# A macaron encoder block in exact split arithmetic: where the operands of down pieces stand among the weight sums, and which three pieces of one group make their sums in place

## The chip, the cores and the metric

The kernel runs on one core of one Trainium2 chip. The metric is the device time of one launch in microseconds. Three runs of the kernel before took 2424.29, 2424.43 and 2427.40 us; the median is 2424.43.

## The reference

One layer on a residual stream of 256 tokens by 2048 channels, all in float32:

```python
x = x + 0.5 * swiglu(rms_norm(x, ffn1_norm), ffn1_w_up, ffn1_w_down)
# HGRN2 and RG-LRU branches of one input projection, merged by gates
x = x + merged @ w_out
x = x + cross_attention(rms_norm(x, xattn_norm), rms_norm(mem, mem_norm), wq, wkv, wo)
x = x + 0.5 * swiglu(rms_norm(x, ffn2_norm), ffn2_w_up, ffn2_w_down)
return rms_norm(x, final_norm)
```

with `swiglu(h, w_up, w_down)`: `gate, up = split(h @ w_up)`, then `(silu(gate) * up) @ w_down`. The hidden width is 5632. The change is only in the two feed-forward blocks, called ffn1 and ffn2 below.

## The kernel before, in words

**Arithmetic.** A float32 product is computed from fp32r halves. Each weight piece of 128 x 2048 numbers (1 MB) is loaded into a `raw` tile and split: ACT copies it into the high part `h` (L138), and DVE subtracts that from `raw` into the low part `l` (L139). TensorE (PE) multiplies high by high (L547), high by the low part of the activations (L548) and low by high (L550).

**Pieces.** The hidden width is worked in 11 groups of 512. A group has eight up pieces, called pairs 0 to 7 by their place in the contraction (256 channels each: two blocks of 128, with four blocks of 512 weights in the piece: gate and up for each of the two). Most pairs use a Strassen-like scheme ("fast") with seven block products in place of eight. For it four *sums* of the weight blocks are needed as well: one operation on DVE for two of them (L285) and one for each of the others (L287, L288; each takes the result in front). They make a second tile `td`, which is split too, in two halves of 1024 columns: ACT writes `h`, DVE `tl`. A fast pair is thus 21 matmuls of 512 columns. When the products of a group are done, they are added up (L634 to L646), pass through silu (L580, L581) and are turned by PE into the operands `hidop` (L592 on ACT, L593 on DVE).

**Down pieces** multiply `hidop` by a 128 x 2048 piece of `w_down`, 24 matmuls each. From group 1 on, two or four of them stand behind each group's eight pairs. They are of kind "plain" (load at L270, split on ACT, split on DVE), but where four stand together the third is "added": it is loaded one piece earlier (L253), ACT writes its negative into `l` (L254), GpSimd's queue adds the weights to that by a DMA (L255), and ACT writes `h` (L263).

**Sums made ahead.** In ffn2, 58 of the pairs are "ready": their sums are made while the middle of the kernel runs (`make_ahead`: a load into `prep`, four subtractions on DVE, L200, and a store to DRAM), and ffn2 loads them as a second 1 MB transfer (L277) beside 768 KB of the piece itself (L275). Which pairs of a group still make their sums *in place* stands in `sums_ready`: in ffn2 group 3, the first behind the attention's last products with its own table entry, pairs 0, 5 and 7. The order of the pairs in each such group is 1, 3, 4, 0, 2, 5, 6, 7, so these are the 4th, 6th and 8th.

**What sets the order.** `weights` keeps two pieces prepared ahead of the one that PE multiplies, and calls `prepare` (from L258) for each. The statements are written in that order, and the recording layer then puts each engine's instructions into a list order of its own by the dependences. `tc.issue_after(x)` holds what is recorded inside it behind `x` in that order; on one engine that is only an order, not a wait. Buffers are few: 3 `raw` (and 2 `raw2` in ffn2, which take two loads of every five), 3 `h`, 3 `l`, and `wide` tiles (`td`, `tl` and the group's `ev` in ffn1). All loads go through SP's queue, each when its buffer is free.

In time, ffn1 runs from 0 to 700 us, the middle to 1723 us and ffn2 to 2416 us.

Of the kernel before, what the change touches and what calls it, by code (L numbers as in the profile page):

```python
# [69 lines left out]

def sums_ready(name, e):

    made = () if e[1] < 3 else (0, 5, 7) if e[1] % 2 else (0, 3, 5, 7)
    return name == "ffn2" and e[0] == "fast" and e[2] not in made


# [1 line left out]
def block_kernel(ctx: ExitStack, tc: tile.TileContext, xT, xin, memT, vec, gfin, bgate, lruw, wu1, wd1, win, wv,  # L78
# [55 lines left out]
    done = {}  # L134


    def split(h, l, raw):
        done["high"] = act.activation(h, raw, ACT.Copy).ins  # L138
        done["low"] = dve.tensor_tensor(out=l, in0=raw, in1=h.bitcast(F32), op=ALU.subtract).ins  # L139
# [5 lines left out]
    plan, ahead, made_ahead = [], [], []  # L145
# [74 lines left out]
    def weights(*key):  # L220
        while plan and len(ahead) < 2:
            i = next(planned)
            k, src, kind = plan.pop(0)
            if i == 0:
                in_turn.enter_context(tc.manual_schedule(engines={sp.engine, act.engine, dve.engine}))
            if i < len(head):
                head[i]()
            if plan and plan[0][2] == "added":
                begun.append(begin_added(plan[0][1]))
            ahead.append((k, prepare(src, kind, 4 if i < 4 else 1)))  # L230
            if i in rest:
                rest[i]()
            beside(i)
            if i == 7:
                in_turn.close()
        k, w = ahead.pop(0)
        assert k == key, (k, key)
        return w
# [16 lines left out]
        nc.gpsimd.dma_start(l, src, accum_op=ALU.add)  # L255
        return raw, l

    def prepare(src, kind, cuts=1):  # L258

        if kind == "added":  # L260
            raw, l = begun.pop(0)
            h = hp.tile([P, 2048], F32R, name="h", tag="h")
            done["high"] = act.activation(h, raw, ACT.Copy).ins  # L263
            return h, l
        raw = raw_tile()
        n = 2048 // cuts
        if kind == "plain":
            h, l = split_tiles()
            for a in range(0, 2048, n):
                sp.dma_start(raw[:, a:a + n], src[:, a:a + n])  # L270
                split(h[:, a:a + n], l[:, a:a + n], raw[:, a:a + n])
            return h, l
        if kind == "ready":
            src, t = src
# [14 lines left out]
        h, l = split_tiles()  # L289
# [10 lines left out]
            tl = lp.tile([P, 2048], F32R, name="tl", tag="l")  # L300
        for a in (0, 1024):
            split(th[:, a:a + 1024], tl[:, a:a + 1024], td[:, a:a + 1024])
        return (h, l), (th, tl)

    def product(xs, *ws, late=()):
# [1010 lines left out]
```

## Time and profile before

| what | value |
|---|---|
| three timed runs | 2424.29, 2424.43, 2427.40 us |
| profiled execution | 2427.28 us, of it the profile's span 2425.5 us |
| granted TensorE clock, mean | 0.998 |
| memory traffic | 684.31 MB, mean 282 GB/s |

The span is what the trace covers; the device time is 1.8 us longer. Rows of the order of time read: start in us, duration in us, engine, line, operation, output and inputs by the program's names, shapes, count, and in square brackets the idle time ahead of it with what ended it. Where several instructions follow each other alike, a row holds them together, and its duration is from the first start to the last end. A row that begins with a stretch (1873.00:1918.20) gives its length and the busy time with the count of instructions of PE, weight loads, DVE, ACT and GpSimd, then the mean granted clock, the busy share of the DMA engines and GB/s. Rows of transfers give the kilobytes of one and the median of the microseconds from issue to landing. Starts of PE instructions are pipelined: two matmuls overlap, so the pitch is the difference of starts.

### The profile page before, as it was taken

Reading aid. Unit: us, or ns where it says so; the run is one execution under the profiler, and the core shown is the slowest. Engines: PE = TensorE matmul, PEld = TensorE weight load, DVE = VectorE, ACT = ScalarE, POOL = GpSimd, SP = SyncE. Lnnn points to the kernel's source line nnn. Section 1 sums busy time; section 2 is a strip of 40 time slices with the busy share of each in tenths; the row PEclk is TensorE's granted clock in tenths of the full one; section 3 lists DMA queues with packets and bytes.
Section 4 is the critical chain, followed back from the end, with each engine's and each line's share of the span. In section 5 each row is a group of like instructions: output and inputs, shape, how many; then the busy total and the mean of one; then the engine's idle time right before and its main releaser. Section 6 shows DMA issues by size and latency. Waiting matters only on the chain.

```text
span 2425.5 us, 30763 instructions
## 1 busy us (share of the span) xinstructions
PE 2409.3 (99%) x12139; PEld 2013.6 (83%) x12139; DVE 2025.6 (84%) x2260; ACT 1455.0 (60%) x1485; POOL 102.2 (4%) x166
## 2 busy tenths in 40 slices
PE   9999999999999999999999999999999999999998
PEld 8888888888788888888888888888888788888887
DVE  7999999998876868779776788777789999999995
ACT  8567677777664454476434555445676666666664
POOL 0000000000000000000000000000000000000000
PEclk9999999999999999999999999999999999999999
DMA  7579999988858776778989889977798878787873
GB/s 294 195 229 287 272 272 270 275 269 268 266 183 323 268 289 241 294 289 323 346 313 349 310 332 354 335 272 263 264 343 308 285 266 293 273 286 276 294 273 144
DMA packets 102385, 684.31 MB, mean 282 GB/s; under 512 B 11361, under 2 KB 11617, under 8 KB 29281
## 3 DMA queue, kind: packets, MB, share of 16 engines
q1 hardware_dynamic: 78192, 518.68, 57.5%
q0 software_dynamic: 23328, 162.54, 22.4%
q8 instruction: 95, 1.56, 0.2%
q10 hardware_dynamic: 720, 1.13, 0.1%
q14 instruction: 50, 0.40, 0.0%
HBM read 619.39 MB, written 62.91 MB: 281 GB/s over the span
## 4 chain that ended last, share of the span: by engine, by line
PE 91%; DVE 3%; DMA 3%; ACT 1%; issue 1%; ACTq 0%; DVEq 0%; SPq 0%
PE acc L547 16%; PE acc L548 16%; PE acc L550 16%; PE acc L313 11%; PE acc L338 8%; PE acc L341 8%; PE acc L339 8%; PE acc L316 6%; DMA raw<-wd 2%; DVE tl L139 1%; ACT h L138 1%; DVE l L139 1%; PE acc L588 1%; PE acc L477 1%; DMA t<-prep 0%
## 5 line engine op out<-in xcount | busy, mean ns | idle before, releaser
L138 ACT ACTIVATE h<-raw 128x2048 fp32r<-128x2048 f32 (+3 forms) x578 | 870.5, 1531 | 620.2 <-PE acc L339 189.6
L139 DVE TENSOR_TENSOR l<-raw,h 128x2048 fp32r<-128x2048 f32 (+2 forms) x406 | 837.3, 2065 | 187.6 <-ACT h L138 186.1
L547 PE MATMUL acc<-h,xh 128*128 128x512 f32 x1241 | 485.2, 392 | 2.7 <-ACT h L138 2.4
L548 PE MATMUL acc<-h,xl 128*128 128x512 f32 x1241 | 483.0, 390 | 0.0
L338 PE MATMUL acc<-h,ops 128*128 128x512 f32 x832 | 326.8, 393 | 0.0
L339 PE MATMUL acc<-h,ops 128*128 128x512 f32 x832 | 324.5, 390 | 0.0
L547 PEld LDWEIGHTS acc<-h,xh 128*128 128x128 f32 x1241 | 233.3, 188 | 56.2 <-ACT h L138 8.0
L547 PE MATMUL acc<-h,hidop 128*128 128x512 f32 x704 | 276.5, 393 | 2.3 <-ACT h L138 2.2
L313 PE MATMUL acc<-ops,h 128*128 128x512 f32 x1152 | 278.2, 393 | 0.0
L548 PE MATMUL acc<-h,hidop 128*128 128x512 f32 x704 | 274.8, 390 | 0.0
L548 PEld LDWEIGHTS acc<-h,xl 128*128 128x128 f32 x1241 | 233.3, 188 | 47.5
L313 PEld LDWEIGHTS acc<-ops,h 128*128 128x128 f32 x1152 | 211.7, 188 | 41.6
L139 DVE TENSOR_TENSOR tl<-raw,h 128x1024 fp32r<-128x1024 f32 x172 | 203.7, 1220 | 14.9 <-ACT h L138 14.5
L341 PE MATMUL acc<-l,ops 128*128 128x512 f32 x832 | 205.8, 389 | 0.0
L550 PE MATMUL acc<-l,hidop 128*128 128x512 f32 x704 | 189.3, 389 | 0.0
L138 ACT ACTIVATE h<-td 128x1024 fp32r<-128x1024 f32 x126 | 131.3, 1057 | 92.9 <-PE acc L548 42.3
L341 PEld LDWEIGHTS acc<-l,ops 128*128 128x128 f32 x832 | 156.2, 188 | 32.4
L338 PEld LDWEIGHTS acc<-h,ops 128*128 128x128 f32 x832 | 156.2, 188 | 32.2
L339 PEld LDWEIGHTS acc<-h,ops 128*128 128x128 f32 x832 | 156.3, 188 | 31.5
L139 DVE TENSOR_TENSOR tl<-td,h 128x1024 fp32r<-128x1024 f32 x126 | 152.0, 1220 | 31.2 <-ACT h L138 31.0
L200 DVE TENSOR_TENSOR prep<-prep 128x512 f32<-128x512 f32 x232 | 159.7, 689 | 20.9 <-DMA prep<-wu 17.1
L550 PE MATMUL acc<-l,xh 128*128 128x512 f32 x645 | 176.4, 389 | 0.0
(242 smaller groups left out, 2739.4 us busy)
## 6 DMA issues: line engine op xcount, KB each, us to landing
raw<-wu SPq DMA_DIRECT2D x114, 1024.0 KB, 6.3
raw<-wd SPq DMA_DIRECT2D x88, 1024.0 KB, 6.3
prep<-wu POOLq DMA_DIRECT2D x58, 1024.0 KB, 7.8
t<-prep POOLq DMA_DIRECT2D x58, 1024.0 KB, 7.8
raw<-t SPq DMA_DIRECT2D x58, 1024.0 KB, 6.9
raw<-wu SPq DMA_DIRECT2D x58, 768.0 KB, 5.0
raw<-win SPq DMA_DIRECT2D x40, 1024.0 KB, 4.8
raw<-wg SPq DMA_DIRECT2D x32, 1024.0 KB, 6.1
```

Source lines behind the costliest of these rows:

```text
L138: done["high"] = act.activation(h, raw, ACT.Copy).ins
L139: done["low"] = dve.tensor_tensor(out=l, in0=raw, in1=h.bitcast(F32), op=ALU.subtract).ins
L200: dve.tensor_tensor(out=b[o], in0=b[x], in1=b[y], op=ALU.subtract)
L313: pe.matmul(acc, h[:, k * P:(k + 1) * P], xs[k], start=k == 0, stop=False)
L316: done["product"] = pe.matmul(acc[:, :T], l[:, k * P:(k + 1) * P], xs[k][:, :T], start=False, stop=k == KT - 1).ins
L338: pe.matmul(accs[t], x[:, t * P:][:, :P], h[j], start=first and j == 0, stop=False)
L339: pe.matmul(accs[t], x[:, T + t * P:][:, :P], h[j], start=False, stop=False)
L341: done["product"] = pe.matmul(accs[t], x[:, t * P:][:, :P], l[j], start=False, stop=last and j == 3).ins
L477: pe.transpose(acc[:, z * T + t * P:][:, :P], tile[:, t * 512 + (2 * y + z) * P:][:, :P], ident)
L547: pe.matmul(acc, ah, bh, start=start, stop=False)
L548: pe.matmul(acc, al, bh, start=False, stop=False)
L550: pe.matmul(acc, ah, bl, start=False, stop=stop)
```

## The change

The first part is a table entry. In group 3 of ffn2 the pairs 2, 4 and 6 make their sums in place (the 3rd, 5th and 7th), and 0, 5 and 7 have theirs made ahead. The number of sums made ahead stays at 58.

The second part is an order. `prepare` remembers, at the end of each piece with sums, the ACT instruction that splits the second half of these sums. The split of a plain down piece is then held behind the latest such instruction. "Added" down pieces are not touched, nor are loads.

```diff
 def sums_ready(name, e):
-    made = () if e[1] < 3 else (0, 5, 7) if e[1] % 2 else (0, 3, 5, 7)
+    made = () if e[1] < 3 else (2, 4, 6) if e[1] == 3 else (0, 5, 7) if e[1] % 2 else (0, 3, 5, 7)
     return name == "ffn2" and e[0] == "fast" and e[2] not in made
...
-            ahead.append((k, prepare(src, kind, 4 if i < 4 else 1)))
+            ahead.append((k, prepare(src, kind, 4 if i < 4 else 1, k[1] == "down")))
...
-    def prepare(src, kind, cuts=1):
+    def prepare(src, kind, cuts=1, down=False):
...
                 sp.dma_start(raw[:, a:a + n], src[:, a:a + n])
-                split(h[:, a:a + n], l[:, a:a + n], raw[:, a:a + n])
+                with tc.issue_after(done["sums"]) if down else ExitStack():
+                    split(h[:, a:a + n], l[:, a:a + n], raw[:, a:a + n])
             return h, l
...
         for a in (0, 1024):
             split(th[:, a:a + 1024], tl[:, a:a + 1024], td[:, a:a + 1024])
+        done["sums"] = done["high"]
         return (h, l), (th, tl)
```

Lines below the edit in `prepare` stand one or two lower in the changed kernel (L634 is L636 there); the split stays at L138 and L139.

**ACT at the end of an ffn1 group.** The rows are the ACT splits of the last two pairs of the first group that has an "added" down piece behind it (`td` is a tile of sums, a `raw` of 2048 a down piece), up to that added piece (L254). Before:

```order
L138 ACTIVATE h<-td 128x1024 x3
L138 ACTIVATE h<-raw 128x1536
L138 ACTIVATE h<-td 128x1024
L138 ACTIVATE h<-raw 128x2048
L138 ACTIVATE h<-td 128x1024
L138 ACTIVATE h<-raw 128x2048
L634 ACTIVATE ev<-acc 128x512
L254 ACTIVATE l<-raw 128x2048
```

and after:

```order
L138 ACTIVATE h<-td 128x1024 x3
L138 ACTIVATE h<-raw 128x1536
L138 ACTIVATE h<-td 128x1024 x2
L138 ACTIVATE h<-raw 128x2048 x2
L636 ACTIVATE ev<-acc 128x512
L254 ACTIVATE l<-raw 128x2048
```

The second half of the last sums has moved ahead of the first down piece; nothing else moved here. On DVE the low part of the down piece likewise stands behind both `tl` splits.

**PE at the end of ffn2 groups 4 to 10.** The rows are the last pair's products (`xh`, `xl` are halves of the activations; `l` and `tl` the low parts of its weights and of its sums) and the first of a down piece (`hidop`). Before:

```order
L550 MATMUL acc<-l,xh 128x512 x3
L550 MATMUL acc<-tl,xh 128x512 x2
L547 MATMUL acc<-h,hidop 128x512
L548 MATMUL acc<-h,hidop 128x512
L547 MATMUL acc<-h,hidop 128x512
L547 MATMUL acc<-h,xh 128x512
L548 MATMUL acc<-h,xl 128x512
L547 MATMUL acc<-h,xh 128x512
L548 MATMUL acc<-h,xl 128x512
L548 MATMUL acc<-h,hidop 128x512
```

and after:

```order
L552 MATMUL acc<-l,xh 128x512 x2
L549 MATMUL acc<-h,xh 128x512
L550 MATMUL acc<-h,xl 128x512
L549 MATMUL acc<-h,xh 128x512
L550 MATMUL acc<-h,xl 128x512
L552 MATMUL acc<-l,xh 128x512
L552 MATMUL acc<-tl,xh 128x512 x4
L549 MATMUL acc<-h,hidop 128x512
```

The two high products on the second half of the sums stood three matmuls into the down piece, and now stand ahead of it, two matmuls into the low products.

**SP's loads in ffn2 group 3, from the third pair to the down pieces.** Names keep their buffer numbers; `t3_4` is the tile of sums made ahead for pair 4 of group 3, a load of 1536 columns from `wu2` is a ready pair, one of 2048 a pair with sums in place, and `wd2` is a down piece (`raw2_15463` the first, `raw_15504` the second). Before:

```order
L275 DMA raw_15247<-wu2 128x1536
L277 DMA raw2_15249<-t3_4_129 128x2048
L279 DMA raw2_15282<-wu2 128x2048
L275 DMA raw_15319<-wu2 128x1536
L277 DMA raw_15321<-t3_2_130 128x2048
L279 DMA raw2_15354<-wu2 128x2048
L275 DMA raw_15391<-wu2 128x1536
L277 DMA raw_15393<-t3_6_131 128x2048
L279 DMA raw_15426<-wu2 128x2048
L270 DMA raw_15504<-wd2 128x2048
L270 DMA raw2_15463<-wd2 128x2048
```

and after:

```order
L280 DMA raw_15247<-wu2 128x2048
L278 DMA raw_15286<-t3_0_129 128x2048
L276 DMA raw2_15284<-wu2 128x1536
L280 DMA raw_15319<-wu2 128x2048
L276 DMA raw2_15356<-wu2 128x1536
L278 DMA raw2_15358<-t3_5_130 128x2048
L280 DMA raw_15391<-wu2 128x2048
L278 DMA raw2_15430<-t3_7_131 128x2048
L276 DMA raw_15428<-wu2 128x1536
L270 DMA raw2_15463<-wd2 128x2048
L270 DMA raw_15504<-wd2 128x2048
```

The pieces with sums in place have exchanged with their neighbours; for pairs 0 and 7 the sums are now loaded ahead of the piece, and the first down piece ahead of the second. In groups 4 to 10 the second down piece is still loaded first.

## The prediction

> **What bounds the kernel now.** I read the page first, then PE's waits, then PE's order of time around the longest of them, then ACT, DVE and SP at the same moments.
>
> ```profile
> PE 2409.3 (99%) x12139; PEld 2013.6 (83%) x12139; DVE 2025.6 (84%) x2260; ACT 1455.0 (60%) x1485; POOL 102.2 (4%) x166
> PE acc L547 <- ACT h L138: 4.6, 5, 2.0
> ```
>
> TensorE (PE) is busy for 99% of the span, and nothing in the change alters what it computes. So the change can only move PE's waits. The view of waits puts nearly all of those that touch this change on one pair: a matmul of L547 waits for a split on ACT (L138), 4.6 us in five waits. In order of time, three of these places in the first feed-forward (ffn1) read:
>
> ```profile
> 255.10 0.39 PE L550 MATMUL acc<-l,xh 128*128 128x512 f32 x1
> 256.01 0.50 PE L547 MATMUL acc<-h,xh 128*128 128x512 f32 x1 [0.53 <-ACT h L138]
> ...
> 379.23 0.39 PE L550 MATMUL acc<-l,xh 128*128 128x512 f32 x1
> 379.66 0.49 PE L547 MATMUL acc<-h,xh 128*128 128x512 f32 x1
> ...
> 626.48 0.39 PE L550 MATMUL acc<-l,xh 128*128 128x512 f32 x1
> 628.53 0.50 PE L547 MATMUL acc<-h,xh 128*128 128x512 f32 x1 [1.66 <-ACT h L138]
> 628.87 0.40 PE L548 MATMUL acc<-h,xl 128*128 128x512 f32 x1
> ```
>
> Unhindered matmuls start 0.227 us apart (three from 2043.36 to 2044.04, quoted below). So the one at 628.53 comes 2.05 - 0.23 = 1.82 us late, and the next start is another 0.11 late (0.34 - 0.23). A wait thus costs some 0.27 us more than the idle time in its brackets. The losses are 0.79, 0.31 and 1.93 us. Whether the change helps depends on what ACT was doing:
>
> ```profile
> 378.54 1.06 ACT L138 ACTIVATE h<-td 128x1024 fp32r<-128x1024 f32 x1 [0.32 <-DVE td L288]
> ...
> 625.62 1.92 ACT L138 ACTIVATE h<-raw 128x2048 fp32r<-128x2048 f32 x1 [2.25 <-DMA raw<-wd]
> 627.44 1.04 ACT L138 ACTIVATE h<-td 128x1024 fp32r<-128x1024 f32 x1
> ```
>
> ```profile
> 253.70 0.69 DVE L288 TENSOR_TENSOR td<-raw,td 128x512 f32<-128x512 f32 x1
> ...
> 377.82 0.69 DVE L288 TENSOR_TENSOR td<-raw,td 128x512 f32<-128x512 f32 x1
> 378.43 2.28 DVE L139 TENSOR_TENSOR l<-raw,h 128x2048 fp32r<-128x2048 f32 x1
> ...
> 625.52 0.69 DVE L288 TENSOR_TENSOR td<-raw,td 128x512 f32<-128x512 f32 x1
> ```
>
> Near 626, and alike near 255, the down piece stands ahead of the second sums split on ACT, and it waits for its load. The sums were ready at 254.39 and 626.21. At 379 ACT is free and it is DVE's own last sum (L288, to 378.51) that is late.
>
> **Part one: the order on ACT.** No instruction is added; two change places.
>
> *Ffn1.* With the sums first, their split ends L288 + 0.04 + 1.06, and PE starts 0.05 behind it (628.48 to 628.53). At 255 that is 254.39 + 1.15 = 255.54, where PE wants 255.33: 0.21 + 0.11 remains of 0.79, a gain of 0.5. At 626: 626.21 + 1.15 = 627.36 against 626.71, so 0.65 + 0.11 remains of 1.93, a gain of 1.2. Around 379, and in the four groups like it, the wait stays: nothing. But the new order hands work back there: the down piece's high part now follows at about 379.5 to 381.4, and its low part on DVE runs 381.45 to 383.74, where the old one began at 378.43 and ended 3.0 us earlier. The first down piece still has its low part in time (PE wants it at 384.5). But its raw tile is free only then, and the fourth piece's load waits for that tile. On ACT the fourth piece's high part (L138) stands ahead of a step of the activation (L580) and of the high part of the third, "added" piece (L263):
>
> ```profile
> 388.57 0.71 ACT L580 ACTIVATE ev<-ev,rtok 128x512 f32<-128x512 f32 x1
> 389.18 1.90 ACT L263 ACTIVATE h<-raw 128x2048 fp32r<-128x2048 f32 x1
> ```
>
> ```profile
> 393.62 0.39 PE L547 MATMUL acc<-h,hidop 128*128 128x512 f32 x1
> ```
>
> The first row of transfers is this group's fourth load, the second the same in the group at 317:
>
> ```profile
> raw<-wd SPq DMA_DIRECT2D x1, 1024.0 KB, 5.9
> ```
>
> ```profile
> raw<-wd SPq DMA_DIRECT2D x1, 1024.0 KB, 5.3
> ```
>
> Issued at 383.75, a load of 5.9 lands at 389.65; 1.83 for its high part, 0.61 for L580 and 1.90 for L263 make 394.0, and PE wants the third piece at 393.62: 0.4 late, where it had 2.5 to spare. With 5.3 it is in time by 0.2. So the cover of the new order is a load of 5.5 us. In the five groups from 317 to 565 these loads took 5.3, 5.9, 5.6, 5.4 and 5.3; the next piece's load now starts 2.2 us behind, not 3.3, and shares the engines for longer. I take 5.7, so 0.2 and a restart of 0.11 in each of five: 1.5 us given back (bounds: nothing at 5.3; 4.5 at 6.3, 0.8 + 0.11 each, the median of the page's row for all these loads). Near 255 and 626 PE comes later after its remaining wait and the cover is 6.2 or more. **Ffn1: 1.7 - 1.5 = 0.2 us gained** (bounds 2.4 gained, 3.6 lost).
>
> *Ffn2, groups 4 to 10.* Here PE's order changes too: the products of the second sums come ahead of the down piece's first three.
>
> ```profile
> 1982.50 0.61 PE L550 MATMUL acc<-tl,xh 128*128 128x512 f32 x2
> 1983.31 0.50 PE L547 MATMUL acc<-h,hidop 128*128 128x512 f32 x1 [0.19 <-ACT h L138]
> ...
> 2043.36 0.84 PE L550 MATMUL acc<-l,xh 128*128 128x512 f32 x3
> 2044.04 0.62 PE L550 MATMUL acc<-tl,xh 128*128 128x512 f32 x2
> ...
> 2348.06 0.61 PE L550 MATMUL acc<-tl,xh 128*128 128x512 f32 x2
> 2348.73 0.50 PE L547 MATMUL acc<-h,hidop 128*128 128x512 f32 x1
> ```
>
> ```profile
> 2042.00 0.69 DVE L288 TENSOR_TENSOR raw<-raw,raw 128x512 f32<-128x512 f32 x1
> ```
>
> Groups 4 and 10 lose 0.35 and 0.21 where the down piece's load was late, and with restarts and a second small wait 0.7 and 0.6. Those 1.3 us go. But the second sums are now wanted two matmuls into the 2043.36 row, at 2043.81, and are ready at 2042.69 + 1.15 = 2043.84. With one restart each that is about 0.15 us in each of seven groups, 1.05 in all. The first down piece, split 1.1 us later, is wanted six matmuls (1.4 us) later. **Groups 4 to 10: 0.25 us gained** (bounds: 2 lost, if each costs 0.45, to 1.3 gained).
>
> **Part two: group 3 of ffn2.** The three pieces with sums made in place become the 3rd, 5th and 7th, not the 4th, 6th and 8th.
>
> ```profile
> 1873.00:1918.20 45.20, 44.64 (x198) 35.76 (x197) 44.51 (x41) 26.67 (x25) 0.00 (x0) 1.00 0.69 256
> 1921.40:1924.90 3.50, 3.50 (x10) 2.69 (x10) 3.50 (x3) 3.50 (x3) 0.00 (x0) 0.52 0.63 194
> ```
>
> ```profile
> 1893.50 1.07 PE L550 MATMUL acc<-tl,xh 128*128 128x512 f32 x4
> ...
> 1915.39 0.50 PE L547 MATMUL acc<-h,xh 128*128 128x512 f32 x1 [0.19 <-ACT h L138]
> ...
> 1917.64 0.73 PE L550 MATMUL acc<-tl,xh 128*128 128x512 f32 x2 [0.37 <-DVE tl L139]
> 1920.41 0.50 PE L547 MATMUL acc<-h,hidop 128*128 128x512 f32 x1 [2.04 <-ACT h L138]
> ```
>
> ```profile
> 1918.45 4.66 ACT L138 ACTIVATE h<-raw 128x2048 fp32r<-128x2048 f32 x3 [1.00 <-DMA raw<-wd]
> ```
>
> Three waits here cost 2.60 us idle and about 0.8 of restarts, and behind them PE runs at a granted clock of 0.52 for 3.5 us, which loses 3.5 x 0.48 = 1.7. That is 5.1 us, the largest loss that the change can reach. The last wait is for the down piece's load. SP issued that load second of two (the order shows it), and now issues it first.
>
> Yet DVE is the floor: it was busy 44.51 of the 45.20 us in the first window, and its set of operations is the same after. In the old order all but one `tl` split of the last piece is done when L288 ends:
>
> ```profile
> 1890.66 0.69 DVE L593 TENSOR_TENSOR hidop<-acc,hidop 128x512 fp32r<-128x512 f32 x1 [0.37 <-ACT hidop L592]
> ...
> 1899.21 3.49 DVE L139 TENSOR_TENSOR tl<-raw,h 128x1024 fp32r<-128x1024 f32 x3
> ...
> 1917.50 0.69 DVE L288 TENSOR_TENSOR raw<-raw,raw 128x512 f32<-128x512 f32 x1
> ```
>
> So the last `tl` ends no earlier than 1918.19 + 1.22 = 1919.4. PE, 13 matmuls past where it stood at 1915.04 without waits, wants it at 1918.0. At least 1.5 us stays. The other bound comes from loads. Pair 5's raw piece takes the buffer of pair 4's sums, which are now made on DVE and freed late: from the L593 that ends at 1891.35, L287, `tl`, L288, `l`, `tl`, `tl` stand ahead, 0.6 + 1.1 + 0.6 + 1.7 + 1.1 + 1.1 = 6.3 us (pitches of the rows here and at 377; the `l` as three quarters of 2.28), so 1897.6.
>
> ```profile
> raw<-t SPq DMA_DIRECT2D x58, 1024.0 KB, 6.9
> raw<-wu SPq DMA_DIRECT2D x58, 768.0 KB, 5.0
> ```
>
> Its load lands at 1902.6 and its split (0.97 us per 1024 columns, 1.5 for 1536) ends at 1904.1; PE, 34 matmuls past 1894.41, wants it at 1902.1: 2.0 late. Its sums (issued 1.1 later, 6.9) land at 1905.6 and are split at 1906.7, eight matmuls on, at 1903.9 + 2.0: 0.8 more. Pair 2's second sums stand behind them on ACT, and pair 6's split waits for a buffer that PE frees only five matmuls before it is wanted: 0.7 and 0.9. Bounds: 1.5 to 4.4. I take 2.5, nearer to the floor, because the old order had hand-overs of the same kind and PE waited there for none until 1915. With 0.3 of restarts, and the clock at full, **group 3 gains 5.1 - 2.8 = 2.3 us** (bounds 3.4 gained, and 1.4 lost with 4.4 of waits, 0.4 of restarts and the half clock again).
>
> The clock is the one place where a rule of the Trainium skill bears on the sum. The row shows half clock behind waits of 0.37 and 2.04 us, and none behind the 1.66 us at 626. The Trainium skill, TensorE: Matmul & The Clock Gate, Part 1: The HAM clock gate, says that the clock falls back to half only after about one idle window of 3.4 us; the trace has the half clock after 2.4 idle us, so the trace decides. By the page none of the new waits could bring it back; by the row one of 2 us or more can, which is the third rival.
>
> **Sum.** 0.2 + 0.25 + 2.3 = 2.75 us against the profiled execution's 2427.3 us: 2424.5. The three timed runs are 2424.3, 2424.4 and 2427.4, so the profiled one stands at the upper of two levels 3 us apart, and the median at the lower. I cannot see where a lower run saves its 3 us; if in group 3, then that group gains nothing there, and the rest makes 2424.4 - 0.45 = 2424.0. Both ways give about the same, and I forecast **2424.2 us**. A measurement here can tell about 0.2% (4.8 us) from no change.
>
> **Rivals.**
> - *All these waits go* (0.2). The places add up to 0.79 + 1.93 + 5 x 0.31 + 5.1 + 1.3 = 10.7 us; if ACT and DVE keep ahead everywhere, 2427.3 - 10.7 = 2416.6. For it: ACT is busy only 60%. Against it: L288 to 378.51 and the 98% of DVE in group 3.
> - *The added piece comes late* (0.2). Its high part stands on ACT behind the fourth piece's load, and the change issues that load 3 us later; from a load of 5.5 us on it decides. At 7.0 us it is 1.5 + 0.11 in each of five groups and some 0.8 near 255 and 626, 9.6 in all, against 1.5 in the sum: 2424.2 + 8.1 = 2432. For it: four of the five loads stood within 0.2 of the cover or over it. Against it: the earlier loads in their old place were all under 6.
> - *The exchange in group 3 brings nothing* (0.15): its waits add up to 4.4, or the half clock returns (1.7 more). The change then does only the first part: 2427.3 - 0.45 = 2426.9.
>
> **How the numbers follow.** The forecast has 0.45, with its own range of 2421 to 2427. Only the first rival is faster by more than 0.2% (below 2419.6): 0.2; only the second is slower (above 2429.3): 0.2; the rest, 0.6, is within 0.2%. The range, 2416.5 to 2430.5, takes in the first rival and the second where its loads take 6.6.
>
> **What would show it.** In the changed profile PE's wait near 626 should be about 0.6 us and the one near 255 about 0.2; the small ones at 317 to 565 should stand as they are, and 14 us behind them PE should wait some 0.2 us for L263 in some groups. In group 3 PE should wait between 1890 and 1920 in several pieces, none of 2 us, with the granted clock at 1.00. In groups 4 to 10 waits on ACT of under 0.1 us should appear ahead of the last sums. PE waits for L263 of 1 us or more would make the second rival right. No PE wait left in group 3 would prove me wrong about DVE as its floor.

## The result, and the profile after

The change takes 2435.34 us, the median of 7 runs (2432.16 to 2437.09). The kernel before, on the same chip, takes 2427.0 us (7 runs, 2424.29 to 2430.33). The ratio is 1.0034 [1.0023, 1.0046], so the whole interval lies above 1 and the change is slower, by 8.3 us between the medians. The profiled span went from 2425.5 to 2430.4 us: the profiled execution is the fastest of the seven (2432.16), so the traces below account for 4.9 us, and what the others lose beyond that was not traced.

The page's row of the engines and PE's waits, which answer to the first two rows of the prediction:

```profile
PE 2410.5 (99%) x12139; PEld 2012.5 (83%) x12139; DVE 2026.1 (83%) x2260; ACT 1452.6 (60%) x1485; POOL 102.2 (4%) x166
```

```profile
PE acc L552 <- DVE tl L139: 6.5, 4, 2.6
PE acc L549 <- ACT h L138: 3.1, 5, 1.5
```

The work of each engine is what it was. PE waits less for ACT, and 6.5 us in four waits for something that cost 0.4 before: the low part of the weight sums (`tl`), which DVE makes. In order of time on PE, ffn1 reads:

```profile
255.23 0.39 PE L552 MATMUL acc<-l,xh 128*128 128x512 f32 x1
255.66 0.50 PE L549 MATMUL acc<-h,xh 128*128 128x512 f32 x1
...
331.41 0.39 PE L549 MATMUL acc<-h,hidop 128*128 128x512 f32 x1
...
358.75 0.50 PE L552 MATMUL acc<-tl,xh 128*128 128x512 f32 x1 [2.26 <-DVE tl L139]
...
383.22 0.50 PE L549 MATMUL acc<-h,xh 128*128 128x512 f32 x1 [1.50 <-ACT h L138]
...
636.51 0.39 PE L552 MATMUL acc<-l,xh 128*128 128x512 f32 x1
636.94 0.50 PE L549 MATMUL acc<-h,xh 128*128 128x512 f32 x1
```

The starts at 255 and 636 are now 0.43 us apart, so the losses at the two places that the change was meant for have shrunk to 0.2 us. The third pieces begin without a wait (331.41 is one). The new waits stand 27 us behind that, inside the *next* group of up pieces: 2.26 us at 358.75, and at its end 1.50 at 383.22. The other new ones are at 424.9 (2.59), 489.9 (1.33) and 513.4 (0.44). One of them is followed by a stretch of half clock, and group 3 of ffn2 has lost its own:

```profile
421.00:429.00 8.00, 5.41 (x18) 4.08 (x17) 6.56 (x5) 4.03 (x3) 0.78 (x1) 0.82 0.42 144
1873.00:1924.00 51.00, 49.50 (x218) 39.45 (x217) 48.76 (x48) 30.95 (x29) 0.00 (x0) 1.00 0.66 250
```

```profile
1899.14 0.50 PE L549 MATMUL acc<-h,xh 128*128 128x512 f32 x1 [0.48 <-ACT h L138]
...
1918.86 0.50 PE L549 MATMUL acc<-h,xh 128*128 128x512 f32 x1 [0.20 <-ACT h L138]
...
1921.09 0.73 PE L552 MATMUL acc<-tl,xh 128*128 128x512 f32 x2 [0.35 <-DVE tl L139]
1922.29 0.50 PE L549 MATMUL acc<-h,xh 128*128 128x512 f32 x1 [0.47 <-ACT h L138]
```

Where the 4.9 us of span come from follows from the starts of all matmuls, which are the same 12139 in both traces: the start of each after is compared with its start before. From 250 to 700 us the change falls 8.23 us behind: 10.4 of new loss between 262 and 622, less 2.2 gained at 255 and 626. Group 3 of ffn2 gained 2.43, the groups behind it 0.16. In the middle, whose code is the same, a wait of 0.9 for DVE (L892) was absent. With 0.13 lost ahead of 250, 8.23 + 0.13 - 0.86 - 2.43 - 0.16 = 4.91.

### The profile page after: what moved, and what is told of

It reads as the page before. It is cut to its first block, busy times and chain, and to the rows that moved or that the text cites. A ratio compares the mean times of both kernels' runs of the same rounds, so it can differ in the third digit from the quotient of the medians.

```text
span 2430.4 us, 30790 instructions
## 1 busy us (share of the span) xinstructions
PE 2410.5 (99%) x12139; PEld 2012.5 (83%) x12139; DVE 2026.1 (83%) x2260; ACT 1452.6 (60%) x1485; POOL 102.2 (4%) x166
## 4 chain that ended last, share of the span: by engine, by line
PE 91%; DVE 4%; DMA 3%; ACT 2%; issue 1%; ACTq 0%; DVEq 0%; SPq 0%
PE acc L549 16%; PE acc L552 16%; PE acc L550 16%; PE acc L315 11%; PE acc L340 8%; PE acc L343 8%; PE acc L341 8%; PE acc L318 6%; DMA raw<-wu 2%; DVE tl L139 1%; DVE l L139 1%; PE acc L590 1%; ACT h L138 1%; PE acc L479 1%; DVE td L286 0%
## 5 line engine op out<-in xcount | busy, mean ns | idle before, releaser
L138 ACT ACTIVATE h<-raw 128x2048 fp32r<-128x2048 f32 (+3 forms) x578 | 869.3, 1531 | 612.5 <-PE acc L341 197.8
L139 DVE TENSOR_TENSOR l<-raw,h 128x2048 fp32r<-128x2048 f32 (+2 forms) x406 | 836.1, 2064 | 185.0 <-ACT h L138 183.4
L549 PEld LDWEIGHTS acc<-h,xh 128*128 128x128 f32 x1241 | 233.5, 188 | 58.5 <-ACT h L138 10.4
L139 DVE TENSOR_TENSOR tl<-raw,h 128x1024 fp32r<-128x1024 f32 x172 | 203.4, 1218 | 21.7 <-ACT h L138 21.3
L138 ACT ACTIVATE h<-td 128x1024 fp32r<-128x1024 f32 x126 | 131.9, 1058 | 108.4 <-DVE td L289 35.6
L139 DVE TENSOR_TENSOR tl<-td,h 128x1024 fp32r<-128x1024 f32 x126 | 152.4, 1219 | 26.8 <-ACT h L138 26.1
```

Source lines behind the costliest of these rows:

```text
L549: pe.matmul(acc, ah, bh, start=start, stop=False)
```

## Where the new waits come from

The pieces of such a group are the pairs 1, 3, 4, 0, 2, 5, 6 and 7, in this order: the first, second and third pair below are 1, 3 and 4, and pair 2 is the fifth piece.

DVE ahead of the wait at 358.75, in the change, and at the same place before:

```profile
345.16 0.68 DVE L289 TENSOR_TENSOR td<-raw,td 128x512 f32<-128x512 f32 x1
...
351.24 1.22 DVE L139 TENSOR_TENSOR tl<-td,h 128x1024 fp32r<-128x1024 f32 x1
...
356.34 1.23 DVE L286 TENSOR_TENSOR td<-raw 128x1024 f32<-128x1024 f32 x1 [3.88 <-DMA raw<-wu]
357.48 1.22 DVE L139 TENSOR_TENSOR tl<-td,h 128x1024 fp32r<-128x1024 f32 x1
```

```profile
343.79 0.69 DVE L288 TENSOR_TENSOR td<-raw,td 128x512 f32<-128x512 f32 x1
...
351.70 1.22 DVE L139 TENSOR_TENSOR tl<-td,h 128x1024 fp32r<-128x1024 f32 x1
352.83 1.22 DVE L285 TENSOR_TENSOR td<-raw 128x1024 f32<-128x1024 f32 x1
353.97 1.22 DVE L139 TENSOR_TENSOR tl<-td,h 128x1024 fp32r<-128x1024 f32 x1
```

The `tl` that PE wants belongs to the third piece and stands in DVE's order behind the first sum (L286) of the next piece with sums, pair 2, and that sum waits 3.88 us for pair 2's load. Before, the load was there and DVE went through. So the load came late; SP's and GpSimd's queues and the view of transfers, in the change, say by how much and why:

```profile
330.85 1.51 SPq L280 DMA_DIRECT2D raw<-wu  x2
...
345.90 0.33 SPq L280 DMA_DIRECT2D raw<-wu  x1
```

```profile
345.81 0.89 POOL L295 DMA_DIRECT2D l<-wu  x1 [4.27 <-ACT l L294]
```

```profile
raw<-wu SPq DMA_DIRECT2D x1, 1024.0 KB, 10.3
l<-wu POOLq DMA_DIRECT2D x1, 768.0 KB, 10.6
```

and before:

```profile
329.23 1.51 SPq L279 DMA_DIRECT2D raw<-wu  x2
...
344.55 0.33 SPq L279 DMA_DIRECT2D raw<-wu  x1
```

```profile
346.26 0.88 POOL L294 DMA_DIRECT2D l<-wu  x1 [4.00 <-ACT l L293]
```

```profile
raw<-wu SPq DMA_DIRECT2D x1, 1024.0 KB, 7.9
l<-wu POOLq DMA_DIRECT2D x1, 768.0 KB, 9.1
```

The load went out 1.35 us later and took 2.4 us longer. The second figure is the larger one. Beside it runs GpSimd's accumulating transfer for the third piece of the group, pair 4 (pairs 3 to 6 are "added" in the same way as the down pieces: ACT writes a negative into `l`, the DMA adds the weights). The quoted texts below call it the transfer of the fourth piece, and one calls the piece ahead of it the third; by the kernels and the order of time they are the third and the second, since the fourth is pair 0, which has no such transfer. Before, the load had a *lead* of 346.26 - 344.55 = 1.71 us on that transfer; now it has -0.09.

Why it went out late is seen on ACT at the start of the group, in the change:

```profile
328.92 1.90 ACT L263 ACTIVATE h<-raw 128x2048 fp32r<-128x2048 f32 x1
...
338.77 1.49 ACT L294 ACTIVATE l<-raw 128x1536 fp32r<-128x1536 f32 x1 [1.52 <-DMA raw<-wu]
340.17 1.06 ACT L594 ACTIVATE hidop<-acc 128x512 fp32r<-128x512 f32 x2
341.12 1.06 ACT L138 ACTIVATE h<-td 128x1024 fp32r<-128x1024 f32 x1
```

and before:

```profile
327.30 1.90 ACT L263 ACTIVATE h<-raw 128x2048 fp32r<-128x2048 f32 x1
...
336.65 2.01 ACT L138 ACTIVATE h<-td 128x1024 fp32r<-128x1024 f32 x2 [3.94 <-PE acc L548]
...
339.51 1.49 ACT L293 ACTIVATE l<-raw 128x1536 fp32r<-128x1536 f32 x1
```

In the new order the negative of the second pair (L294) stands ahead of the second half of the first pair's sums; before, it stood behind it. It waits for the second pair's load, which SP issued at 330.85 and not at 329.23, each time 0.03 us behind the end of L263 (330.82, before 329.20): the load takes the raw tile that the high part of the added down piece gives back, and L263 stands on ACT behind the high part of the fourth down piece, whose load had waited for the late low part of the first. The first pair's `tl`, the second pair's last sum (L289, ended at 345.84) and the release of its raw tile follow late, and pair 2's load is the one that waits for this tile.

The theory that came out of this (**E** in the quoted texts): the price is not the lateness itself but the lost lead. When the load is issued with or behind the accumulating transfer, the load takes 9 to 12 us beside it, DVE waits for the load, and PE waits behind DVE. (What the two transfers share was not taken apart.) Its forerunners and rivals were: **A**, the price is DVE's order, the `tl` behind a sum that waits; **B**, something else is late anyway; **C**, the late low part of the first down piece is enough to start it; **F**, the order on ACT at the group's start costs by itself. What each experiment's quoted text says of its theories stands with it.

## The experiments

Each ratio is to the kernel before, run beside it on the same chip. There its medians were 2425.2 (experiments 1 to 4), 2426.43 (5 to 8), 2425.24 (9 to 11) and 2426.19 us (12).

**1 and 2: each part alone.** The order alone keeps the old table entry:

```diff
-    made = () if e[1] < 3 else (2, 4, 6) if e[1] == 3 else (0, 5, 7) if e[1] % 2 else (0, 3, 5, 7)
+    made = () if e[1] < 3 else (0, 5, 7) if e[1] % 2 else (0, 3, 5, 7)
```

> The changed kernel with the old three pairs (0, 5, 7) in group 3 of ffn2, so the held split of the down pieces alone. The trace of the change puts 10 us of new PE waits into ffn1 (near 356, 381, 422, 488 and 512 us) and takes 3.2 us out of group 3. Theory A, the order alone makes the loss in ffn1: slower than the change by what group 3 then loses again, 1.5 to 3 us, so some 10 us above the kernel before. Rival, the loss needs both parts: within 3 us of the kernel before.

Measured: 2440.25 us (6 runs, 2434.51 to 2446.45), 1.0060 [1.0044, 1.0076]. Its waits on PE:

```profile
PE acc L552 <- DVE tl L139: 9.0, 4, 3.6
PE acc L552 <- DMA l<-wd: 2.3, 1, 2.3
```

The loss is in the order, with `tl` waits in ffn1 as in the change; the rival (within 3 us of before) falls. The trace is 11.3 us longer than the change's, and the starts of the matmuls say where: 6.1 us in the last ffn1 group, where pair 2's load has a lead of 0.02 us against 1.06 there in the change's trace, and 4.3 us behind group 3 of ffn2, where a down piece waits 2.29 for its accumulating transfer (the second row, ended at 1957.2) and a half clock follows. Nothing in the trace ties either of them to the old table entry.

The exchange alone is the kernel before with `(2, 4, 6) if e[1] == 3 else` in the table:

> The kernel before with pairs 2, 4 and 6 in group 3 and no held split. Theory A: ffn1 stays as before, and group 3 of ffn2 gains most of what it gained in the change, so 2 to 3.5 us below the kernel before. Rival, the exchange alone gains nothing because the late down piece still stands ahead of the last sums: within 0.7 us of before.

Measured: 2423.66 us (11 runs, 2421.94 to 2426.49), 0.9990 [0.9982, 0.9999]. In its trace group 3 has waits of 0.48, 0.36, 0.20 and 0.89 us. A gain of 2.4 us by the ratio agrees with the 2.3 of the prediction; the interval (0.2 to 4.4) doesn't fix its size, and it does not exclude the rival's 0.7 either.

**3: the order in ffn2 only**, with the exchange:

```diff
-            ahead.append((k, prepare(src, kind, 4 if i < 4 else 1, k[1] == "down")))
+            ahead.append((k, prepare(src, kind, 4 if i < 4 else 1, k[1] == "down" and k[0] == "ffn2")))
```

> The changed kernel with the down pieces' split held only in ffn2. Theory A: ffn1 runs as before, group 3 gains 3 us and groups 4 to 10 about 0.3, so 3 to 4 us below the kernel before and 11 to 12 below the change. Rival, the loss comes from the exchange or from ffn2: as slow as the change.

Measured: 2423.47 us (11 runs, 2422.3 to 2427.25), 0.9994 [0.9985, 1.0003]. The new waits of ffn1 are gone. So what the change loses, it loses by the order of ffn1's down pieces. The expected 3 to 4 us below the kernel before did not show: it is 1.5 by the ratio, and the interval reaches from 3.6 below to 0.7 above.

**4: the wanted `tl` ahead of the waiting sum.** The first sum of pair 2 is held, in seven ffn1 groups, behind the `tl` of the pair in front. This only turns two neighbours on DVE:

```diff
+            ahead.append((k, prepare(src, kind, 4 if i < 4 else 1, k[1] == "down",
+                                      k[:2] == ("ffn1", "fast") and k[2] > 3 and k[3] == 2)))
...
+            with tc.issue_after(done["tl"]) if behind else ExitStack():
+                dve.tensor_tensor(out=two[0], in0=raw[:, None, :512].broadcast_to([P, 2, 512]), in1=two[1],
+                                  op=ALU.subtract)
...
+        done["tl"] = done["low"]
```

> The changed kernel, with one pair of rows exchanged on DVE in seven ffn1 groups: the second low split of the third pair's sums (tl) stands ahead of the first sum of the pair two pieces on (pair 2), which waits there for its load. Everything else stands as in the change. Theory A, the tl that PE wants is stuck behind a sum that waits for its transfer: PE's waits near 356, 422 and 488 go (2.4, 2.75 + 1.6 of half clock, 1.5) and with them most of the later ones at the end of these groups (1.7 and 0.6), so 6 to 10 us below the change. Rival B, the transfers as such are too late and PE would wait for pair 2 itself: within 2 us of the change.

Measured: 2432.46 us (12 runs, 2426.09 to 2438.45), 1.0026 [1.0017, 1.0035]: by the ratio 2 us better than the change (1.0034 [1.0023, 1.0046]; its repeat in 11 has 1.0026 too), which is within the noise. A expected 6 to 10, B at most 2, so B's time came.

```profile
PE acc L552 <- ACT h L138: 6.2, 5, 2.5
PE acc L555 <- DMA l<-wu: 1.6, 2, 0.9
```

The long `tl` waits are gone, and waits of 2.49 us at the ends of two groups (to 383.9 and 513.8) have come instead: the load is late for everything behind it. DVE's order is where the wait shows, and not its cause. A falls as the whole story, and the question became why the load is late.

**5: the trigger alone.** The kernel before, with only the low part of the first down piece in a set of four in ffn1 (`late`) behind the last `tl` on DVE:

```diff
+        with tc.issue_after(behind) if behind is not None else ExitStack():
+            done["low"] = dve.tensor_tensor(out=l, in0=raw, in1=h.bitcast(F32), op=ALU.subtract).ins
...
+                split(h[:, a:a + n], l[:, a:a + n], raw[:, a:a + n], done["tl"] if late else None)
```

> The kernel before; in the ffn1 groups with four down pieces the low part of the first of them stands on DVE behind the last low split of the sums (tl), as in the change, while ACT and the queues keep their order. The raw tile of the first down piece thus comes free some 2.4 us later than before. Theory C, the late raw tile delays the loads of the fourth down piece and of the next group's first pairs, and the delay goes round the ring of three raw tiles: 4 to 12 us above the kernel before, with PE waits for tl some 35 us behind the down pieces. Rival D, it is the order on ACT that costs: within 2 us of before.

Measured: 2425.29 us (11 runs, 2420.63 to 2437.34), 1.0000 [0.9988, 1.0012]. The leads stayed at 1.72, the loads took 6.6 to 9.1. The late low part as made here doesn't start the chain, and C falls for it; D's time came. It is a somewhat weaker trigger than the change's, though: the fourth down piece's load is held back by 2.4 us (from 2.2 us behind the added piece's load to 4.6, against 5.2 in the change), and the first loads of the next groups took 6.0 to 7.1 us, against 7.6 to 9.2. That the order at the start of the next group is needed too rests on 10.

**6 and 7: the accumulating transfers, one kind at a time.** Two kernels are the change with accumulating transfers in ffn1 cut short. The first moves 256 of 2048 columns for the added down pieces, the second 256 of 1536 for the added pairs; the rest of these low parts is left out of the computation, and all else stands as it was.

```diff
-                nc.gpsimd.dma_start(l, src, accum_op=ALU.add)
+                n = 256 if "xd" in scoped else 2048
+                nc.gpsimd.dma_start(l[:, :n], src[:, :n], accum_op=ALU.add)
```

> The changed kernel, in ffn1 with the accumulating transfer of the third (added) down piece cut from 2048 to 256 columns; the other columns of its low part keep the negative copy, so this part of the result is left out. Theory C1, the next group's first load (9.1 us in the change near 324, 4.9 before) is slow because it now starts together with this transfer: that load is back at 5 to 6 us and the kernel 5 to 9 us below the change. Rival C2, it is the collision further on (pair 2's load with a pair's own accumulating transfer, 10.3 us near 346) or the late issue alone: within 3 us of the change.

Measured: 2425.67 us (11 runs, 2422.88 to 2427.72), 0.9994 [0.9985, 1.0003]. The first loads of each group took 5.9 to 7.3 us (7.6 to 9.2 in the change; their lead over the added down piece's transfer is -0.06 us in both), the leads of pair 2's loads came back to 1.07 but for one of 0.42, and these took 5.9 to 7.6. The loss is gone here too (0.9994 against 1.0034 is 10 us), as C1 had it and C2 not: the first loads, slowed beside the added down piece's transfer, are a link of the chain.

```diff
-            nc.gpsimd.dma_start(l[:, 512:], src[:, 512:], accum_op=ALU.add)
+            nc.gpsimd.dma_start(l[:, 512:768], src[:, 512:768], accum_op=ALU.add)
```

> The changed kernel, in ffn1 with the accumulating transfers of the added pairs cut from 1536 to 256 columns; the other columns of these low parts keep the negative copy, so this part of the result is left out. Theory C2, pair 2's load is slow because it starts together with such a transfer: it falls from 10 to about 6 us, the waits near 356, 422 and 488 go, and the kernel is 6 to 10 us below the change. Rival C1, the delay comes from the first load: its 9 us stay and the kernel is within 4 us of the change.

Measured: 2423.05 us (11 runs, 2420.79 to 2426.99), 0.9989 [0.9980, 0.9998]. SP's and GpSimd's queues, and the transfers:

```profile
345.84 0.33 SPq L280 DMA_DIRECT2D raw<-wu  x1
```

```profile
345.56 0.88 POOL L295 DMA_DIRECT2D l<-wu  x1 [4.10 <-ACT l L294]
```

```profile
raw<-wu SPq DMA_DIRECT2D x1, 1024.0 KB, 4.9
l<-wu POOLq DMA_DIRECT2D x1, 128.0 KB, 5.9
```

Pair 2's load is issued as late as in the change (345.84 against 345.90), again behind the other transfer, and it takes 4.9 us, not 10.3. The loss is gone, though the first loads of the groups, whose transfer beside them is whole here, still took 7.7 to 11.3 us; C1 alone falls. A late issue by itself is harmless, and so is a slow first load; the transfer beside pair 2's load is not.

**8: the order only where a wait was seen to go.** As in 3, and with the first down piece behind the last ffn1 group:

```diff
-            ahead.append((k, prepare(src, kind, 4 if i < 4 else 1, k[1] == "down")))
+            ahead.append((k, prepare(src, kind, 4 if i < 4 else 1, k[1] == "down" and (k[0] == "ffn2" or k[2:] == (7, 2, 2, 7)))))
```

> The changed kernel with the down pieces' split held in ffn2 and, in ffn1, only for the first down piece behind the last group, where no further pair follows that could come late (the wait of 1.66 us near 626 in the trace before). Theory A and C: 1.5 us below the kernel that holds only in ffn2, so about 3 us below the kernel before. Rival: the loads of the last down pieces come late in place of it, no better than holding in ffn2 alone (1.7 below before).

Measured: 2425.27 us (11 runs, 2421.49 to 2428.05), 0.9992 [0.9983, 1.0001]. There is no wait near 626 in the trace, but there is none in the third run's trace either, whose ffn1 has the old order; so this can't be credited to the edit. Against the third run (0.9994) the time can't tell.

**9: give the lead back from the other side.** The change with the negative of the third piece (pair 4) on ACT, on which its accumulating transfer waits, held behind the first half of the second piece's sums; in the order that came out it stands behind both halves. The two neighbours of experiment 4 came out turned on DVE as well, though its edit is not in this kernel.

```diff
+            with tc.issue_after(done["half"]) if behind else ExitStack():
+                act.activation(l[:, 512:], raw[:, 512:], ACT.Copy, scale=-1.0)
...
             split(th[:, a:a + 1024], tl[:, a:a + 1024], td[:, a:a + 1024])
+            if not a:
+                done["half"] = done["high"]
```

> The kernel of the run with tl first, and in seven ffn1 groups one more exchange, on ACT: the negative copy (L294) of the fourth piece of the group, behind which its accumulating transfer starts, stands behind the first half of the third piece's sums instead of ahead of it, so that this transfer starts about 1 us later. In the traces so far, pair 2's load takes 6.6 to 9.8 us where it is issued 0.4 us or more ahead of that transfer and 9.4 to 11.8 us where it is not. Theory E, the lead decides: the lead is back at 0.7 to 1.2 us, pair 2's load at 7 to 9 us, the PE waits for tl and at the ends of the groups go, and the kernel is 5 to 8 us below the run with tl first, so at or 1 to 2 us under the kernel before. Rival, the load is late in any case because its tile comes free late: no better than the run with tl first (2432).

Measured: 2427.32 us (11 runs, 2423.78 to 2432.26), 1.0012 [1.0003, 1.0020], where 4 had 1.0026. The queues at the same place:

```profile
345.78 0.33 SPq L281 DMA_DIRECT2D raw<-wu  x1
```

```profile
348.60 0.88 POOL L297 DMA_DIRECT2D l<-wu  x1 [7.19 <-ACT l L296]
```

The load goes out as late as in the change. The lead is now 2.8 to 3.8 us, more than the planned 1, the loads take 5.0 to 7.8, and the `tl` and end-of-group waits are gone. But the accumulating transfer itself now lands late: PE waits 1.91, 0.61, 0.79 and 1.49 us for it (L556 for `l`). E holds for the load, and the edit moves some of the price to the other party: the kernel is 3.4 us better by the ratios than 4, where 5 to 8 were expected.

**10: the order at the group's start.** The change with the second pair's negative (L294) back behind the first pair's sums on ACT:

```diff
+            with tc.issue_after(done["sums"]) if behind else ExitStack():
+                act.activation(l[:, 512:], raw[:, 512:], ACT.Copy, scale=-1.0)
```

> The changed kernel, in ffn1 with the negative copy of the second piece of a group behind both halves of the first piece's sums on ACT, as in the kernel before; on DVE the first sum of that second piece then stands behind the turn of the hidden values, also as before. Theory E, only the lead of pair 2's load over the transfer behind it decides: the tile for that load comes free at 347.0 in place of 345.8 and the transfer starts at about 346.9, so the lead is -0.2 us in most groups, and the kernel is as slow as the change or up to 8 us slower. Rival F, the new order at the start of a group is itself the loss: back to within 3 us of the kernel before.

Measured: 2426.58 us (11 runs, 2422.53 to 2436.78), 1.0011 [0.9999, 1.0023]. My expectation under E was a lead of -0.2, because I had let the raw tile come free at 347.0; it was free at 345.3, and the leads were 1.07 in five of the six groups. The time is the one that F named, yet it came by way of the lead: the one group in which it was 0.25 (469.7) had a load of 10.4 us and waits of 1.99 and 0.49 on PE, and the others had none over 0.5. F and E agree on the order at the start as a cause; this run doesn't tell them apart by the time, and the one group speaks for E. The traced execution (2424.9) is one of the faster; four of the eleven took over 2430.

**11: the change once more**, without an edit:

> The change as it is, beside the other two on one chip, with a second trace. Theory E: 2432 to 2438 us, and in the trace PE waits for tl of over 1 us in just those groups in which pair 2's load is issued less than 0.4 us ahead of the fourth piece's accumulating transfer. Rival: waits for tl also in groups with a longer lead, or none in groups without.

Measured: 2432.15 us (12 runs, 2427.55 to 2438.92), 1.0026 [1.0016, 1.0036]. The six leads were 1.07, -0.08, 0.80, -0.07, 0.94 and 1.07, the loads 7.3, 11.5, 8.4, 10.7, 9.9 and 10.1. PE's `tl` waits were 3.38 and 2.58 in the two groups with a lead below zero, and 0.77 and 0.89 in the last two, whose loads took some 10 us with a lead of about 1. The order of the leads repeats the first profile of the change (1.06, -0.09, 0.15, -0.12, 1.07, 1.06), the third lead apart. E's limit of 1 us holds, but the rival is right in part: shorter waits came at leads of 0.94 and 1.07 too, so the lead is not all that sets the load's duration.

**12: take the lead from the kernel before.** Only DVE's order is touched: in seven ffn1 groups the last sums of the second pair stand behind a residual add (L662), and one of them is made twice, so that the raw tile comes free later and pair 2's load goes out with the accumulating transfer.

```diff
+            with tc.issue_after(done["residual"]) if late else ExitStack():
+                for _ in range(2 if late else 1):
+                    dve.tensor_tensor(out=td[:, 1024:1536], in0=raw[:, 1024:1536], in1=td[:, :512], op=ALU.subtract)
```

> The kernel before, without any of the change; in seven ffn1 groups, on DVE alone, the last two sums of the second pair stand behind a residual add (L662) instead of ahead of it, and one of them (L287) is made twice. The raw tile that pair 2's load takes comes free 1.3 to 1.9 us later, so the load is issued 0.4 us ahead of the fourth piece's accumulating transfer to 0.2 us behind it, where it was 1.7 us ahead. Theory E, losing this lead is enough: pair 2's load takes 8 to 11 us, PE waits for tl 35 us behind the down pieces in several groups, and the kernel is 3 to 10 us above the kernel before. Rival F, the lead is not enough, other parts of the change's order are needed: within 2 us of before, with no wait for tl over 0.5 us.

Measured: 2457.0 us (5 runs, 2452.29 to 2461.18), 1.0127 [1.0108, 1.0146].

```profile
354.99 0.33 SPq L280 DMA_DIRECT2D raw<-wu  x1
```

```profile
354.60 0.88 POOL L297 DMA_DIRECT2D l<-wu  x1 [3.99 <-ACT l L296]
```

```profile
raw<-wu SPq DMA_DIRECT2D x1, 1024.0 KB, 9.9
l<-wu POOLq DMA_DIRECT2D x1, 768.0 KB, 10.5
```

```profile
365.40 1.23 DVE L286 TENSOR_TENSOR td<-raw 128x1024 f32<-128x1024 f32 x1 [4.13 <-DMA raw<-wu]
366.54 1.22 DVE L139 TENSOR_TENSOR tl<-td,h 128x1024 fp32r<-128x1024 f32 x1
```

```profile
PE acc L553 <- DVE tl L139: 19.6, 9, 3.1
PE acc L550 <- ACT h L138: 8.3, 8, 2.5
```

All six leads measured are -0.39 us, the loads take 9.9 to 10.9, and every one of the seven groups has a `tl` wait of 2.3 to 3.1. The rows repeat the change's chain without its order on ACT: a late load that has lost its lead is enough. The size, 30.8 us or 4.4 per group, is above the 3 to 10 in all that I had expected: waits at the ends of groups come on top, and the half clock behind four of the long waits in ffn1. The seven sums made twice add 0.6 us of DVE each. The load is late here as well as without its lead; how late, in the group shown, is told from the load of the added down piece (L253): pair 2's load is issued 27.7 us behind it in the kernel before, 29.5 in the change, 29.7 in 7, 29.8 in 9 and 29.9 here. As late as here, but with no large transfer beside it (7) or with a lead (9), it took 4.9 and 7.2 us and brought no `tl` wait. What the later order on DVE costs by itself was not measured.

Over all traces here in which nothing is left out, that of experiment 9 aside, pair 2's loads in the six ffn1 groups from 283 us on sort by their lead:

| lead, us | loads | us to landing: range, median | waits of PE behind them |
|---|---|---|---|
| below 0.3 | 17 | 9.4 to 11.8, 10.6 | in all 17, 0.7 to 3.6 us |
| 0.3 to 1.1 | 19 | 6.2 to 10.1, 7.8 | in 3, 0.4 to 0.9 |
| 1.7 | 30 | 6.5 to 10.2, 6.9 | in 1, 0.25 |

## Why the prediction was wrong, point by point

- **The waits at 255 and 626** (1.7 us gained): the number came, 2.2, but the runs don't credit it to the order. In the traces of 3 and 5, where ACT has the old order there, these two places are shorter than in the trace of before by the same 0.5 and 1.6, and by 0.4 and 1.7: the down piece's load landed earlier against PE's work, and PE waited 0.2 us at most. In 2, also in the old order, 1.3 us are left at 626, and in the repeat of the change 0.4 at 255. How much is lost there varies from one execution to the next, and the prediction took one trace for the rule.
- **What the new order hands back** (1.5 us, at the third, added piece): this is the step that failed. The fourth down piece's loads took 4.8 or 4.9 us in five of six groups and 6.0 in one, so all but one were under the cover of 5.5, and PE never waited for L263. The prediction followed the late L263 to PE only, and put at nothing the load that waits for the tile which L263 gives back. The delay went on through the release of tiles: L263 and with it the second pair's load 1.6 us later, L294 ahead of the sums on ACT, pair 2's load 1.35 later, and there it met the accumulating transfer; PE paid 27 us behind the place that I priced. Not 1.5 but 10.4 us were given back. The wait near 379, which I left at 0.31, grew to the 1.50 at 383.22; I read that as DVE held up by the same load, and in 6 and 7, where the loads are quick, it is absent. The prediction's bounds for ffn1 (2.4 gained, 3.6 lost) are wider than the terms beside them give (1.7 gained, 4.5 - 1.7 = 2.8 lost); the measured 8.2 lies outside both.
- **The order at a group's start** was not in the prediction at all. The order of the instructions shows L294 moved ahead of the second half of the first pair's sums, and I counted only the instructions at the group's end. Experiment 10 puts it back, and the leads return in two of the three groups in which the change's profile had lost them.
- **Group 3 of ffn2** (2.3 gained): right, with 2.4, waits of 0.2 to 0.5 in several pieces, and the clock at 1.00. DVE stayed the floor: 48.76 busy of 51.00 us. How much of it is the exchange's is less sure. In two of the four traces with the old table entry (1 and 5) the group is 2.2 and 2.0 us shorter than in the trace of before too, with waits of up to 0.96 and 1.66 and no half clock in it; in the ten traces with the new entry it is 2.1 to 3.1 shorter. So a good part of the 2.4 is a half clock that comes in some executions of the old kernel and was seen in none with the exchange. (The six pitches in the prediction's working add up to 6.2 as printed, not 6.3, which moves nothing.)
- **Groups 4 to 10** (0.25 gained): right within what can be seen, 0.16.
- **The second rival** (2432 by the added piece) named nearly the time by chance, and not the place: no wait for L263 is in the trace. "All these waits go" failed with the new ones. The third rival's price, a half clock from a new wait of 2 us or more, was paid in ffn1, behind 2.59 but not behind 2.26, and not in group 3.
- **The two levels, 3 us apart:** the wait at L892 in the middle, in code that no kernel here changes, was 0.9 us in the trace of before, none in the change's, 3.1 in that of the second run and 2.9 and 3.0 in those of 3 and 8; these three executions were among the three slowest of their eleven. This can be what separates single runs; it was not tested. The 29 runs of the kernel before beside experiments 1 to 4 fill the stretch from 2423.1 to 2428.2 evenly (one took 2430.6), so there are no two levels.

Shown by the runs: the loss is in ffn1's order (1, 2, 3); with either accumulating transfer cut short it is gone (6, 7); an equally late load costs nothing where the collision is absent (7) and brings no `tl` wait where it has a lead (9); taking the lead away from the kernel before brings the loss (12). Argued from traces, with 6 and 10 as support: the steps from the late low part to the late issue. Open: why a lead of about 1.07 gives loads of 6.2 as well as 10.1 us, and why one and the same kernel loses the lead in other groups in another execution (11 against the change's first profile). A fourth raw tile in ffn1, which would take the issue off this path, wasn't tried.

No run beats the kernel before clearly: the exchange alone, 0.9990 [0.9982, 0.9999], is the best that computes everything.

## What to carry to other kernels

A delay that costs nothing where it is made must be followed through the tile that it frees, the load that waits for this tile, and whatever transfer runs when that load then goes out; here PE noticed nothing for a whole set of down pieces and then lost 10.4 us, where 1.5 had been priced. When an edit holds an instruction back on an in-order engine, compare the order a whole round of the loop further on, and price every pair of neighbours that has changed places. A load's duration from the old trace is only good for the old time of issue: look at what else is in flight at the new one. And a wait seen in one trace may be missing in another with the same order there, as those at 255 and 626 were: a gain that rests on one trace is not certain.

## What the runs showed of the hardware that was not expected

A plain load of 1 MB beside an accumulating transfer of 768 KB took 6.9 us (median) with a lead of 1.7 us and 10.6 with less than 0.3; with the accumulating transfer cut to 128 KB it took 4.9 to 5.6, whatever the lead (-0.79 to 1.07). So some 1.5 us of issue were worth 3.7 us of landing.

The half clock, for 3.4 us each time, came with single waits in the two feed-forward blocks of 2.59 us (the window from 421 above, where it stood from 426.1 to 429.5), of 3.38 in the repeat, of 2.29 in the first run, of 2.49 twice in the fourth, and of 2.84, 2.50, 3.11, 2.50 and 2.07 in the last; with 3.59 and 3.03 in the first run it stood for 6.8 us. It did not come with 2.26 in the change, 2.05 in the first run, 2.58 in the repeat, nor with 2.89, 2.53, 2.31 and 2.70 in the last run. So the length of the wait alone doesn't decide it between 2.0 and 2.9 us.
